# Stick-breaking attention: the running sums' products five units behind the softplus split instead of four, tiles five and six units apart

## The chip, the cores and the metric

The kernel runs on one core of one Trainium2 chip. The metric is the time of one execution in device microseconds; where a kernel is run several times, the median counts. A profiled execution stands beside these runs: its trace is what the sections below read.

## What is computed

One inference step of a one-layer hybrid decoder, for one prompt (16 meta tokens and 1024 tokens, together T = 1040) and for 8 sample sequences of 4 tokens with a paged cache. The input, normalised, goes through one shared input projection. Half of its columns feed a stick-breaking attention of 8 heads of size 128, the other half a gated linear attention; both go through gates and a shared output projection. The attention of the prompt is the part that the change touches. Its weights are not a softmax over keys but a product of "breaks", computed with running sums:

```python
def stick_break_weights(z, mask):
    sp = jnp.where(mask, jax.nn.softplus(z), 0.0)
    later = lax.cumsum(sp, axis=z.ndim - 1, reverse=True) - sp
    return jnp.where(mask, jnp.exp(jax.nn.log_sigmoid(z) - later), 0.0)

def sb_attend(qb, qpos, k, v, kpos, bias):
    a = stick_break_weights(sb_logits(qb, k, bias), kpos[None, :] < qpos[:, None])
    return jnp.einsum('bhqk,bkhd->bqhd', a.astype(v.dtype), v)
```

So key tile j of a block of queries needs the sum of the softplus values over all later key tiles: the tiles of one block form a chain, from the last key tile to the first.

All matrix products are made in fp32 accuracy out of three products of a number's two parts: the value rounded to the matmul's format (the "hi" part, a cast on ACT) and what is left of it (the "lo" part, a subtraction on DVE).

## The kernel before, in words

**Stages.** First the input is normalised and transposed; then come, head by head, the projections of the 8 attention heads with their attention woven in (from about 100 to 770 us); then the low-rank part of the gate and three groups of gate columns, with the last head's attention (to about 870 us); then the gated linear attention and the output projection. The attention of the sample sequences (its products and sums are the DVE instructions of L464, `jk`) is spread over DVE through all of it.

**Units.** A head's projection is `inproj` (L331), for v, then k, then q. Each has 8 loop steps over weights (a fresh weight chunk every second step: the hi cast on ACT at L182, the lo subtraction on DVE at L185), and each step has three column chunks of 384, 384 and 304 columns (for q 368, 384 and 304, without the 16 meta columns): six matmuls a chunk, L342 to L344 twice. After each chunk `W.beat()` runs. A chunk of six matmuls is one unit of the kernel's clock. A projection has 24 units and a head 72.

**Weaving.** `Weaver` (L53) holds generators with a due unit; at each beat it resumes those whose unit has come, and what they issue lands on the engines right behind the unit just made. The order on each engine follows that, but for steps marked `urgent` (weight casts, the projections' evacuations), which a scheduler may pull ahead as soon as their data are there.

**Attention.** Two units after head h's q projection, `attend` (L631) is started; it runs beside the projections of head h + 1. It starts 14 tiles, in the ORDER of L641: query block 1 (columns 528 to 1040, 512 queries) with key tiles 8 down to 0, then query block 0 with key tiles 4 down to 0. The tiles are numbered 0 to 13 in this order below. Their widths n are 32, 158, 284, 410 and five times 512 for block 1, then 24 to 512 (150, 276, 402, 512 among them) for block 0. The start of the next tile follows 2 to 5 units later, by n (L638).

A tile (`attend_tile`, L578) goes through these steps:

- z, three products (L589 to L591); DVE adds the bias and clips (L595); ACT exp and ln (L596, L597); DVE the maximum (L598): X is now the softplus. Where the diagonal passes through, POOL masks (L601). Then it waits 2 units.
- It waits until the previous tile of its block has set `carry`, units at a time. ACT copies the row of sums of the previous tile into row 0 of X (L607); `split_tmp` makes hi_s (ACT, L574) and lo_s (DVE, L575) out of X. Then it waits D1 units.
- The running sums' products: L610 (hi_s) and L611 (lo_s) add the triangular matrix's products to z. `carry` is set. ACT makes the weight Y (exp, L615); POOL masks (L617, diagonal tiles); hi_a and lo_a are split from Y. Then it waits D2 units.
- The three products with V into O (L623 to L625). The last tile of a block copies O to `ost` (ACT, L628) and stores it to DRAM (L629, `od`).

**Buffers.** X, Y and ost share three buffers (tag X), hi has three, lo has three, z has four. V, k and q of a head have one buffer each (a hi and a lo tile). So the reload of V for head h + 1 (`load_v`, L554: loads into staging tiles, three ACT copies L566 and three DVE subtractions L568) must wait for the last product with V of head h; the copies of head h + 1's k into its tile (`split_k`, ACT L693, DVE L694) must wait for the last z of head h; q is written by the evacuation of its projection (ACT L715, DVE L716, and L718 for the sample tokens). The projections' accumulators `acc` have three buffers: a chunk's next use waits for the evacuation of three chunks before.

**Queues.** Every engine works its instructions in the order in which they stand: ACT's and DVE's order around a tile is what the change moves. Weight loads, V's loads and the stores of od go through SP's queue.

Of the kernel before, what the change touches and what calls it, by code (L numbers as in the profile page):

```python
# [84 lines left out]
def hybrid_step(ctx: ExitStack, tc: tile.TileContext, x_prompt, x_sample, cache_k, cache_v, state_gla,  # L85
# [104 lines left out]
    with tc.tile_pool(name="xp", bufs=2) as xp, tc.tile_pool(name="xps", bufs=5, space=PSUM) as xps:  # L190
# [109 lines left out]
        for c, (lo, hi) in enumerate(XCHUNKS):  # L300
            n = hi - lo
# [225 lines left out]
    with tc.tile_pool(name="sp", bufs=1) as sp, tc.tile_pool(name="sps", bufs=1, space=PSUM) as sps:  # L527
# [103 lines left out]
        def attend(h, q, kt, V):  # L631

            carry, O = {}, {}
            for qi, j in ORDER:
                qlo, qhi = ((16, 528), (528, REAL))[qi]
                n = qhi - max(qlo, j * KT)
                W.spawn(attend_tile(h, qi, qlo, qhi, j, (qhi - 1) // KT, q, kt, V, carry, O))
                yield 2 if n < 100 else 3 if n < 200 else 4 if n < 450 else 5  # L638

        D1, D2 = 4, 6  # L640
        ORDER = [(1, j) for j in range(8, -1, -1)] + [(0, j) for j in range(4, -1, -1)]  # L641

        def values(h, behind):
# [19 lines left out]
        def head(h):  # L663
# [56 lines left out]
            inproj(C_SQ + h * P, ev_q, META, f"q{h}")  # L720
            V = values(h, copied[-1])
            W.spawn(attend(h, qt, kt, V), 2)

        W.spawn(z_feed(lambda n: 2), lasting=True)
# [946 lines left out]
def build(arrays_by_name):  # L1671
    import concourse.bacc as bacc
    nc = bacc.Bacc("TRN2", target_bir_lowering=False, num_devices=1, dynamic_dma_scratch_size=256)
    arrays, args = {}, []
    for name in _INS:
        a = arrays_by_name[name]
        arrays[f"in_{name}_dram"] = a
        args.append(nc.dram_tensor(f"in_{name}_dram", a.shape, mybir.dt.from_np(a.dtype), kind="ExternalInput").ap())
    for i, shape in enumerate(_OUTS):
        args.append(nc.dram_tensor(f"out_{i}_dram", shape, F32, kind="ExternalOutput").ap())  # L1680
    with tile.TileContext(nc) as tc:
        hybrid_step(tc, *args)
    return nc, arrays
# [8 lines left out]
```

## Time and profile before

| | |
|---|---|
| time, median of 3 runs | 2067.45 us (2066.13 to 2067.91) |
| the profiled execution's own time | 2066.38 us |
| its span, first to last instruction | 2064.6 us |
| mean granted TensorE clock | 0.999 |
| PE busy | 2024.8 us (98%) |
| PEld busy (weight loads) | 1863.6 us (90%) |
| DVE busy | 1552.7 us (75%) |
| ACT busy | 953.4 us (46%) |
| POOL busy | 84.6 us (4%) |

PE is TensorE's matmul part and PEld its weight load, which runs beside the matmul before it. Their shares say how full TensorE's queue is; a matmul's end is modelled, so that a stall shows as a longer distance from start to start, with only a part of it listed as idle time. The span leaves 2066.38 - 2064.6 = 1.78 us around it. The groups and rows of a view read `engine line operation output<-inputs shape`, with the time in us, and in square brackets the engine's idle time before it and what ended that.

### The profile page before, as it was taken

Reading aid. Unit: us, or ns where it says so; the run is one execution under the profiler, and the core shown is the slowest. Engines: PE = TensorE matmul, PEld = TensorE weight load, DVE = VectorE, ACT = ScalarE, POOL = GpSimd, SP = SyncE. Lnnn points to the kernel's source line nnn. Section 1 sums busy time; section 2 is a strip of 40 time slices with the busy share of each in tenths; the row PEclk is TensorE's granted clock in tenths of the full one; section 3 lists DMA queues with packets and bytes.
Section 4 is the critical chain, followed back from the end, with each engine's and each line's share of the span. In section 5 each row is a group of like instructions: output and inputs, shape, how many; then the busy total and the mean of one; then the engine's idle time right before and its main releaser. Section 6 shows DMA issues by size and latency. Waiting matters only on the chain.

```text
span 2064.6 us, 41985 instructions
## 1 busy us (share of the span) xinstructions
PE 2024.8 (98%) x12507; PEld 1863.6 (90%) x12507; DVE 1552.7 (75%) x6282; ACT 953.4 (46%) x2293; POOL 84.6 (4%) x304
## 2 busy tenths in 40 slices
PE   6999999999999999999999999999999999999998
PEld 5999999999999998999999999998888898788776
DVE  7368989888988989899798897978544347454576
ACT  7355555565655656433534335343433325332332
POOL 0012000101000000000000000000000000000000
PEclk9999999999999999999999999999999999999999
DMA  6354454544455442533433433335776666452485
GB/s 202 103 139 148 139 159 133 171 132 147 146 160 146 140 124 76 139 102 82 108 100 79 125 82 110 98 82 155 236 233 231 220 222 200 139 166 74 129 271 202
DMA packets 371821, 301.85 MB, mean 146 GB/s; under 512 B 42360, under 2 KB 312104, under 8 KB 371592
## 3 DMA queue, kind: packets, MB, share of 16 engines
q1 hardware_dynamic: 371288, 298.64, 48.6%
q8 instruction: 98, 1.61, 0.3%
q14 instruction: 131, 1.07, 0.2%
q10 hardware_dynamic: 304, 0.53, 0.1%
HBM read 241.75 MB, written 57.31 MB: 145 GB/s over the span
## 4 chain that ended last, share of the span: by engine, by line
PE 75%; DVE 12%; DMA 6%; ACT 3%; issue 3%; SPq 0%; POOL 0%; DVEq 0%; ACTq 0%; POOLq 0%
PE acc_g L342 5%; PE acc_g L343 5%; PE acc_g L344 5%; DVE jk L464 5%; PE b L1593 4%; PE b L1595 4%; PE b L1594 4%; PE acc_k L342 3%; PE acc_k L344 3%; PE acc_k L343 3%; PE acc_v L342 2%; PE acc_q L342 2%; PE acc_q L344 2%; PE acc_q L343 2%; PE acc_v L344 2%
## 5 line engine op out<-in xcount | busy, mean ns | idle before, releaser
L464 DVE SCALAR_TENSOR_TENSOR jk<-kp,qb 128x128 f32<-128x128 f32 x2048 | 593.8, 290 | 43.5 <-DMA qb<-qsd 1.7
L342 PE MATMUL acc_g<-hT,wh_g 128*128 128x368 f32 (+2 forms) x768 | 251.4, 327 | 0.5 <-DVE ga L389 0.5
L343 PE MATMUL acc_g<-hT,wh_g 128*128 128x368 f32 (+2 forms) x768 | 247.6, 322 | 0.0
L344 PE MATMUL acc_g<-hT,wl_g 128*128 128x368 f32 (+2 forms) x768 | 247.1, 322 | 0.0
L1593 PE MATMUL b<-ring,f 128*128 128x512 f32 x416 | 164.3, 395 | 3.5 <-ACT gx L521 1.4
L464 DVE DVE_READ_ACCUMULATOR jk<-kp,qb 128x1 f32 x2048 | 167.6, 82 | 0.0
L1594 PE MATMUL b<-ring,f 128*128 128x512 f32 x416 | 162.6, 391 | 0.0
L1595 PE MATMUL b<-ring,f 128*128 128x512 f32 x416 | 162.1, 390 | 0.0
L342 PEld LDWEIGHTS acc_g<-hT,wh_g 128*128 128x128 f32 x768 | 144.5, 188 | 13.3 <-issue 10.8
L343 PEld LDWEIGHTS acc_g<-hT,wh_g 128*128 128x128 f32 x768 | 144.6, 188 | 1.1 <-issue 0.4
L1395 DVE TENSOR_TENSOR ring<-wr,ring 128x512 fp32r<-128x512 f32 x104 | 71.3, 689 | 98.4 <-ACT ring L1394 97.7
L344 PEld LDWEIGHTS acc_g<-hT,wl_g 128*128 128x128 f32 x768 | 144.5, 188 | 0.0
L342 PE MATMUL acc_gv<-hT,wh_gv 128*128 128x400 f32 (+2 forms) x384 | 130.5, 340 | 0.0
L1394 ACT CAST ring<-wr 128x512 fp32r<-128x512 f32 x104 | 64.1, 620 | 139.3 <-PE b L1595 77.0
L342 PE MATMUL acc_k<-hT,wh_k 128*128 128x384 f32 (+1 forms) x384 | 126.4, 329 | 0.0
L343 PE MATMUL acc_gv<-hT,wh_gv 128*128 128x400 f32 (+2 forms) x384 | 125.3, 326 | 0.0
L342 PE MATMUL acc_q<-hT,wh_q 128*128 128x368 f32 (+2 forms) x384 | 125.1, 326 | 0.0
L344 PE MATMUL acc_gv<-hT,wl_gv 128*128 128x400 f32 (+2 forms) x384 | 124.8, 325 | 0.0
L344 PE MATMUL acc_k<-hT,wl_k 128*128 128x384 f32 (+1 forms) x384 | 124.7, 325 | 0.0
L343 PE MATMUL acc_k<-hT,wh_k 128*128 128x384 f32 (+1 forms) x384 | 124.5, 324 | 0.0
L344 PE MATMUL acc_q<-hT,wl_q 128*128 128x368 f32 (+2 forms) x384 | 123.4, 321 | 0.0
L343 PE MATMUL acc_q<-hT,wh_q 128*128 128x368 f32 (+2 forms) x384 | 123.4, 321 | 0.0
(454 smaller groups left out, 5294.3 us busy)
## 6 DMA issues: line engine op xcount, KB each, us to landing
kp<-in_cache_k_dram SPq DMA_DIRECT2D x512, 64.0 KB
vr<-in_cache_v_dram SPq DMA_DIRECT2D x64, 512.0 KB
tf<-in_w_out_dram SPq DMA_DIRECT2D x64, 256.0 KB
td<-tf SPq DMA_DIRECT2D x64, 256.0 KB
qb<-qsd SPq DMA_DIRECT2D x64, 256.0 KB
wr_g<-in_w_in_dram SPq DMA_DIRECT2D x64, 256.0 KB
wr<-td SPq DMA_DIRECT2D x56, 256.0 KB
wr<-in_w_out_dram SPq DMA_DIRECT2D x48, 256.0 KB
```

Source lines behind the costliest of these rows:

```text
L342: mm(acc[c][:, :n], wh, hh[k][:, lo:hi], start=(k == 0), stop=False)
L343: mm(acc[c][:, :n], wh, hl[k][:, lo:hi], start=False, stop=False)
L344: W.mark = mm(acc[c][:, :n], wl, hh[k][:, lo:hi], start=False, stop=(k == NK - 1)).ins
L464: ins = vec.scalar_tensor_tensor(jk[:], kp[:], 1.0, qbs[h, b][:, t, :], ALU.mult, ALU.mult, accum_out=zt[:, t, NPG - 1 - i:NPG - i])
L1394: act.copy(wh, r)
L1395: vec.tensor_tensor(wl, r, wh.bitcast(F32), ALU.subtract)
L1593: mm(bk[:], ah, wh, start=first and k == 0, stop=False, skip_group_check=True)
L1594: mm(bk[:], ah, wl, start=False, stop=False, skip_group_check=True)
L1595: mm(bk[:], al, wh, start=False, stop=last and k == 7, skip_group_check=True)
```

## The change

Two lines in `attend`: D1 is 5 instead of 4, and where the next tile started 4 or 5 units after a tile of at least 200 columns, it starts 5 or 6 units after it.

```diff
-                yield 2 if n < 100 else 3 if n < 200 else 4 if n < 450 else 5
+                yield 2 if n < 100 else 3 if n < 200 else 5 if n < 450 else 6
-        D1, D2 = 4, 6
+        D1, D2 = 5, 6
```

No instruction is added or removed on any engine; they stand in another order. With D1 = 5 the links of a block's chain are at least 5 units apart, and a head's last running sums and last products with V come at units 146 and 152, counted from the start of its v projection, where they came at 134 and 140. The next head's own first z is at unit 146 (two after its q projection) in both. So a head's last tiles now stand among the next head's first ones. Three places show what that does to ACT's and DVE's rows. Names carry head, query block and key tile: X2_1_8 is X of head 2, block 1, key tile 8 (tile 0); then comes a buffer number.

**First place: ACT, tiles 11 and 12 of head 1** (block 0, key tiles 2 and 1), with the copies of head 2's k (`k0_2`) and one weight cast between them. Before:

```order
L182 CAST wh_q2_2_4579<-wr_q2_2_4577 128x512
L693 CAST k0_2_3660<-kraw2_2_4259 128x114
L693 CAST k0_2_3660<-kraw2_2_4259 128x126
L693 CAST k0_2_3660<-kraw2_2_4259 128x32
L596 ACTIVATE X1_0_0_4418<-X1_0_0_4418 128x512
L545 COPY st_k2_2_4431<-tk_k2_2_4430 128x256
L597 ACTIVATE X1_0_0_4418<-X1_0_0_4418 128x512
L546 COPY st_k2_2_4431<-tk_k2_2_4430 48x128
L615 ACTIVATE Y1_0_2_4442<-z1_0_2_4176,bias0_827 128x276
L607 ACTIVATE X1_0_1_4311<-z1_0_2_4176 1x276
L574 CAST hi_a1_0_2_4445<-Y1_0_2_4442 128x276
L574 CAST hi_s1_0_1_4451<-X1_0_1_4311 128x402
```

After:

```order
L693 CAST k0_2_3643<-kraw2_1_4160 128x2x126
L693 CAST k0_2_3643<-kraw2_2_4204 128x114
L693 CAST k0_2_3643<-kraw2_2_4204 128x126
L693 CAST k0_2_3643<-kraw2_2_4204 128x32
L596 ACTIVATE X1_0_0_4574<-X1_0_0_4574 128x512
L597 ACTIVATE X1_0_0_4574<-X1_0_0_4574 128x512
L615 ACTIVATE Y1_0_2_4614<-z1_0_2_4324,bias0_827 128x276
L607 ACTIVATE X1_0_1_4472<-z1_0_2_4324 1x276
L574 CAST hi_a1_0_2_4617<-Y1_0_2_4614 128x276
L574 CAST hi_s1_0_1_4622<-X1_0_1_4472 128x402
L182 CAST wh_v3_0_4797<-wr_v3_0_4795 128x512
```

The copies of k stood ahead of tile 13's exp (L596 of X1_0_0); they still do. Y of tile 11 (L615 of Y1_0_2) and hi_s of tile 12 (hi_s1_0_1) follow in the same order; on PE, L610 and L611 of tile 12, which hi_s and lo_s feed, stand five units behind those of tile 11 instead of four. Tile 13's z was made at unit 125 and tile 11's L611 at 126; now they are made at 134 and 136.

**Second place: ACT, from head 1 to head 2**: the last ost of head 1, the evacuations of head 2's q, the copies of head 2's V (`V0_2`) and head 2's first tiles. Before:

```order
L628 COPY ost1_0_4731<-O1_0_4377 128x512
L715 ACTIVATE q0_2_4269<-acc_q2_0_4272 128x368
L715 ACTIVATE q0_2_4269<-acc_q2_1_4273 128x384
L182 CAST wh_v3_1_4967<-wr_v3_1_4965 128x512
L715 ACTIVATE q0_2_4269<-acc_q2_2_4274 128x272
L566 CAST V0_2_4808<-vr2_0_4825 128x384
L566 CAST V0_2_4808<-vr2_1_4856 128x384
L718 ACTIVATE qsm2_4271<-acc_q2_2_4274 128x32
L566 CAST V0_2_4808<-vr2_2_4896 128x384
L596 ACTIVATE X2_1_8_4865<-X2_1_8_4865 128x32
L597 ACTIVATE X2_1_8_4865<-X2_1_8_4865 128x32
```

After:

```order
L596 ACTIVATE X2_1_6_4995<-X2_1_6_4995 128x284
L597 ACTIVATE X2_1_6_4995<-X2_1_6_4995 128x284
L566 CAST V0_2_4790<-vr2_0_4807 128x384
L566 CAST V0_2_4790<-vr2_1_4847 128x384
L566 CAST V0_2_4790<-vr2_2_4890 128x384
L628 COPY ost1_0_5010<-O1_0_4529 128x512
L182 CAST wh_v3_3_5237<-wr_v3_3_5235 128x512
L615 ACTIVATE Y2_1_8_5022<-z2_1_8_4852,bias0_827 128x32
L607 ACTIVATE X2_1_7_4921<-z2_1_8_4852 1x32
L574 CAST hi_a2_1_8_5025<-Y2_1_8_5022 128x32
L574 CAST hi_s2_1_7_5050<-X2_1_7_4921 128x158
```

The copies of V and ost stood ahead of tile 0's exp; they now stand behind the ln of tile 2 (X2_1_6), with Y of tile 0 (Y2_1_8), the row of sums for tile 1 and hi_s of tile 1 behind them and behind a weight cast. Two of the three X buffers hold X2_1_7 and X2_1_6 at this place, whose splits are still to come, so that Y2_1_8 takes the third, which ost1_0 has until its store to DRAM has been read out. Before, Y2_1_8 stood 19 rows behind ost1_0; now it stands two behind it.

**Third place: DVE, the evacuations of head 2's q** (L716, `q1_2`), beside tiles 12 and 13 of head 1 and a weight's lo part (`wl_v3_1`). Before:

```order
L464 SCALAR_TENSOR_TENSOR jk0_1_2_3_4758,zt0_1_4675<-kp0_1_2_4549,qb0_1_4467 128x128
L489 TENSOR_TENSOR tf2_1_4332<-tf2_1_4332 128x512
L716 SCALAR_TENSOR_TENSOR q1_2_4270<-acc_q2_0_4272,q0_2_4269 128x368
L464 SCALAR_TENSOR_TENSOR jk0_1_3_0_4790,zt0_1_4675<-kp0_1_3_4589,qb0_1_4467 128x128
L464 SCALAR_TENSOR_TENSOR jk0_1_3_1_4792,zt0_1_4675<-kp0_1_3_4589,qb0_1_4467 128x128
L716 SCALAR_TENSOR_TENSOR q1_2_4270<-acc_q2_1_4273,q0_2_4269 128x384
L464 SCALAR_TENSOR_TENSOR jk0_1_3_2_4794,zt0_1_4675<-kp0_1_3_4589,qb0_1_4467 128x128
L489 TENSOR_TENSOR tf2_1_4332<-tf2_1_4332 128x512
L716 SCALAR_TENSOR_TENSOR q1_2_4270<-acc_q2_2_4274,q0_2_4269 128x272
```

After:

```order
L575 TENSOR_TENSOR lo_a1_0_1_4712<-Y1_0_1_4708,hi_a1_0_1_4711 128x402
L716 SCALAR_TENSOR_TENSOR q1_2_4215<-acc_q2_0_4217,q0_2_4214 128x368
L464 SCALAR_TENSOR_TENSOR jk0_1_2_1_4728,zt0_1_4646<-kp0_1_2_4499,qb0_1_4415 128x128
L575 TENSOR_TENSOR lo_s1_0_0_4736<-X1_0_0_4574,hi_s1_0_0_4735 128x512
L716 SCALAR_TENSOR_TENSOR q1_2_4215<-acc_q2_1_4218,q0_2_4214 128x384
L185 TENSOR_TENSOR wl_v3_1_4962<-wr_v3_1_4959,wh_v3_1_4961 128x512
L716 SCALAR_TENSOR_TENSOR q1_2_4215<-acc_q2_2_4219,q0_2_4214 128x272
L464 SCALAR_TENSOR_TENSOR jk0_1_2_2_4730,zt0_1_4646<-kp0_1_2_4499,qb0_1_4415 128x128
L489 TENSOR_TENSOR tf2_1_4283<-tf2_1_4283 128x512
L464 SCALAR_TENSOR_TENSOR jk0_1_2_3_4732,zt0_1_4646<-kp0_1_2_4499,qb0_1_4415 128x128
```

Before, only the sample attention's rows (L464, `jk`, and L489) stood between them, since the splits of tiles 12 and 13 were long done; now lo_a of tile 12 stands ahead of the first and lo_s of tile 13 ahead of the second.

## The prediction

> **What bounds the kernel now.** I read the page's busy shares first, then the waits of TensorE's two parts over the stretch that the change touches (100 to 870 us), then one of these waits in time, on every engine that takes part.
>
> ```profile
> PE 2024.8 (98%) x12507; PEld 1863.6 (90%) x12507; DVE 1552.7 (75%) x6282; ACT 953.4 (46%) x2293; POOL 84.6 (4%) x304
> PEclk9999999999999999999999999999999999999999
> ```
>
> TensorE is busy for 98% of the span at a full clock, and the change takes no matmul away. It can only win time in which TensorE stands. The two tables of waits say how much that is, first for the matmuls, then for the weight loads:
>
> ```profile
> PE z L611 <- DVE lo_s L575: 2.5, 9, 0.8
> PE z L610 <- ACT hi_s L574: 1.7, 4, 0.9
> PE acc_g L342 <- DVE ga L389: 0.5, 1, 0.5
> ```
>
> ```profile
> PEld z L611 <- DVE lo_s L575: 6.2, 13, 1.1
> PEld z L610 <- ACT hi_s L574: 3.3, 5, 1.2
> PEld acc_g L342 <- DVE ga L389: 0.7, 1, 0.7
> ```
>
> The columns are total us, number of waits, longest. All that TensorE waits for attention are the two splits of the softplus, the operands of L610 and L611: 4.2 us by the matmuls, 9.5 by the weight loads. Which of them the time pays shows in one event, in head 1 at tile 12 (matmuls, then weight loads):
>
> ```profile
> 284.25 0.33 PE L343 MATMUL acc_q<-hT,wh_q 128*128 128x368 f32 x1
> 284.42 0.32 PE L344 MATMUL acc_q<-hT,wl_q 128*128 128x368 f32 x1
> 284.83 0.45 PE L610 MATMUL z<-hi_s,ntri 128*128 128x402 f32 x1
> 285.45 0.45 PE L611 MATMUL z<-lo_s,ntri 128*128 128x402 f32 x1 [0.17 <-DVE lo_s L575]
> 285.74 0.34 PE L342 MATMUL acc_q<-hT,wh_q 128*128 128x384 f32 x1
> ```
>
> ```profile
> 284.83 0.19 PEld L610 LDWEIGHTS z<-hi_s,ntri 128*128 128x128 f32 x1 [0.39 <-ACT hi_s L574]
> 285.44 0.19 PEld L611 LDWEIGHTS z<-lo_s,ntri 128*128 128x128 f32 x1 [0.43 <-DVE lo_s L575]
> ```
>
> Undisturbed, the next 368-column matmul starts 0.17 us later; 402 columns are worth 0.17 x 402/368 = 0.19. Here the starts are 0.41 and 0.62 apart: 0.24 + 0.43 = 0.67 us lost, against 0.82 in the weight loads' rows and 0.17 in the matmuls'. So the price of all these waits is near 0.67/0.82 x 9.5 = 7.8 us; 4.2 and 9.5 are its bounds.
>
> Why the splits are late there, ACT's and DVE's rows show:
>
> ```profile
> 280.57 0.60 ACT L693 CAST k<-kraw 128x114 fp32r<-128x114 f32 x3
> 281.08 0.62 ACT L596 ACTIVATE X<-X 128x512 f32<-128x512 f32 x1
> 281.87 0.63 ACT L597 ACTIVATE X<-X 128x512 f32<-128x512 f32 x1
> 282.54 0.49 ACT L615 ACTIVATE Y<-z,bias 128x276 f32<-128x276 f32 x1
> 284.26 0.52 ACT L574 CAST hi_s<-X 128x402 fp32r<-128x402 f32 x1
> ```
>
> ```profile
> 284.81 0.58 DVE L575 TENSOR_TENSOR lo_s<-X,hi_s 128x402 fp32r<-128x402 f32 x1
> ```
>
> ACT works without a gap through the copies of the next head's k and tile 13's exp and ln before it comes to tile 11's Y at 282.54; the row of sums and hi_s follow, and lo_s ends at 285.39. This is a queue in front of a short chain, not a slow chain.
>
> **What the change does to it.** The distance between one L610 and the next grows from four units to five. A unit of six matmuls is 6 x 0.17 = 1.03 us, one of 304 columns 1.03 x 304/368 = 0.85. The longest wait in the tables is 1.2, so one unit takes away nearly all of each. At tile 12 there is more to it: tile 13's z comes one unit before tile 11's L611 in the old order and two units before it in the new one, so the work that held Y up has a further unit to drain. I take both rows at L610 and L611 as gone: -7.8 (bounds -4.2 and -9.5).
>
> What is added lies at the changes of head, seven of them. There tile 0's Y and tile 1's splits now follow the V copies and ost. These rows have the durations, and a tile 0 to tile 1 link from head 4 has the chain behind Y (ACT, then DVE):
>
> ```profile
> L566 ACT CAST V<-vr 128x384 fp32r<-128x384 f32 x24 | 11.1, 509 | 1.9 <-DMA vr<-out_dram 1.8
> L628 ACT COPY ost<-O 128x512 f32<-128x512 f32 x16 | 9.4, 586 | 16.0 <-PE O L625 15.8 <-DVE lo_a L575 0.2
> ```
>
> ```profile
> 498.00 0.27 ACT L615 ACTIVATE Y<-z,bias 128x32 f32<-128x32 f32 x1
> 498.77 0.32 ACT L574 CAST hi_s<-X 128x158 fp32r<-128x158 f32 x1
> ```
>
> ```profile
> 499.12 0.32 DVE L575 TENSOR_TENSOR lo_s<-X,hi_s 128x158 fp32r<-128x158 f32 x1
> ```
>
> From Y's start to lo_s's end it is 499.44 - 498.00 = 1.44 us. Let s be the start of the last product with V of a head. Tile 1's L611 stands six units behind it: four units of 1.03 and two of 0.85, that is 5.8 us, and with L625 itself (0.17 x 512/368 = 0.24), tile 3's three z products of 410 columns (3 x 0.19) and L610 it is due at about s + 6.7. On ACT the last product has ended by about s + 0.4; three V copies of 0.51 and ost of 0.59 take it to s + 2.5. Y must then wait until ost has been stored, since it gets ost's buffer. With a landing time L of that store, lo_s is ready at s + 2.5 + L + 1.44, and TensorE stands for L - 2.8 us where that is positive.
>
> L is what the trace does not have at this place. Three pairs of rows bound it (a store's issue on SP, and the instruction that waited for it or used its buffer):
>
> ```profile
> 852.62 0.32 SPq L629 DMA_DIRECT2D od<-ost  x1
> 856.52 0.30 ACT L800 CAST wal<-walr 96x128 fp32r<-96x128 f32 x1 [1.82 <-DMA od<-ost]
> ```
>
> ```profile
> 2056.47 0.33 SPq L1567 DMA_DIRECT2D out_dram<-og  x1
> 2058.74 1.67 POOL L1580 TENSOR_TENSOR y<-y,xr 128x512 f32<-128x512 f32 x1 [327.25 <-DMA out_dram<-og]
> ```
>
> ```profile
> 179.03 0.34 SPq L629 DMA_DIRECT2D od<-ost  x1
> 182.47 0.37 ACT L615 ACTIVATE Y<-z,bias 128x150 f32<-128x150 f32 x1
> ```
>
> The first store took 3.9 us to release its waiter, the second 2.3, and the third, in the middle of a head, at most 3.4, since Y shows no wait. So a head's change costs between 0 and 1.1 us. I take 2.8 for six of the seven, which is about the middle of 2.3 and 3.4 and costs nothing, and 3.9 for one: +1.1 in all (bounds 0 and 7 x 1.1 = 7.7).
>
> [...]
>
> Two smaller terms. The wait of L342 for `ga` (0.5 to 0.7 us in the rows above) lies at the end of the low-rank part, where tiles of head 7 now stand between what fills and what empties the accumulator: it about doubles, +0.5 (bounds 0 and 0.7). And in head 7 the last tiles of block 1 have their splits behind other work more closely than before; no row shows them waiting, and two waits of the size of the longest listed, 1.2, bound it: 0 to 2.4, taken as +1.0.
>
> The sum: -7.8 + 1.1 + 0.5 + 1.0 = -5.2. Against the profiled execution's 2066.38 that is 2061.2 us. The median of the runs lies 1.07 higher, at 2067.45: 2062.25 us for it. 0.2% of 2067.45 is 4.1 us, about what a measurement of this kernel can tell from no change.
>
> **The rivals.** *No change, because the stores give it back.* ACT works in order, and holds all behind an instruction that waits for a DMA; the trace has such a case, a V copy in head 4 with a short copy behind it that had nothing to do with it:
>
> ```profile
> 492.70 0.51 ACT L566 CAST V<-vr 128x384 fp32r<-128x384 f32 x1 [1.75 <-DMA vr<-out_dram]
> 493.12 0.17 ACT L658 COPY zns<-zn 32x32 f32<-32x32 f32 x1
> ```
>
> If each of the seven stores lands in 3.9 us, they cost 7.7 instead of 1.1: -7.8 + 7.7 + 1.5 = +1.4, so 2068.85 us. For it speaks that the landing of 3.9 is the only one of od which the trace shows to the end; against it the 3.4 in mid-head, where Y went into a stored ost's buffer without a wait. [...]
>
> *Slower, by the evacuation of q.* DVE's part of it (L716) now stands behind lo_a of tile 12 and lo_s of tile 13, and the accumulator that it frees is the next chunk's of the next head's v. The prices:
>
> ```profile
> L575 DVE TENSOR_TENSOR lo_s<-X,hi_s 128x512 fp32r<-128x512 f32 x48 | 32.9, 685 | 0.1
> L716 DVE SCALAR_TENSOR_TENSOR q<-acc_q,q 128x384 fp32r<-128x384 f32 x8 | 4.5, 558 | 0.5 <-ACT q L715 0.5
> L575 DVE TENSOR_TENSOR lo_a<-Y,hi_a 128x402 fp32r<-128x402 f32 x8 | 4.6, 574 | 0.0
> ```
>
> Where lo_a waits for its hi part, L716 waits with it. If both splits, 0.57 + 0.69 us, come on top of an evacuation that was just in time, a head loses 1.26 us, eight heads 10.1: -5.2 + 10.1 = +4.9, so 2072.35 us. It decides from about 0.9 us of lateness: two units lie between a chunk's last use for q and its accumulator's first for v, 1.03 + 0.85 = 1.88 us, and L716 with an ACT half of about its own length takes 1.0 of them. Against it: L342 of v shows no wait for L716 in the tables, and of the two splits ahead of L716 the second, lo_s of tile 13, needs nothing that is late.
>
> *The waits stay.* The k copies keep their place ahead of tile 13's exp in the new order, and move along with it. If Y of tile 11 is held up by a unit more as well, nothing at L610 and L611 is won, and the small terms remain: +1.1 + 1.5 = +2.6, so 2070.05 us. Against it stands that z of tile 13 comes two units ahead of L611 now.
>
> **How the numbers follow.** The forecast 0.50, 2062.25 us; its own range goes from -9.5 with no costs to -4.2 + 1.1 + 0.5 + 1.0 = -1.6, that is 2058 to 2066. No change by the stores 0.30, slower by q 0.15, the waits staying 0.05. Of the forecast's chance a tenth, 0.05, lies above 2063.3, where the gain is under 0.2%, and of the stores' case a tenth, 0.03, above 2071.6. Faster: 0.45. Within 0.2%: 0.05 + 0.27 + 0.05 = 0.37. Slower: 0.15 + 0.03 = 0.18. The range reaches from 2058.5 (-9.5 with 0.5 of the costs) to 2069.5 (the stores' case and half of the 1.4 by which it loses), and leaves out q's and, by a hair, the waits staying.
>
> **What would show it.** In the profile of the changed kernel, the rows of L610 and L611 among TensorE's waits should be under 1.5 us in the weight loads, with nothing left at tile 12. At the head changes, ACT's Y of tile 0 shows a wait for the od store or none, and L611 of tile 1 a wait of L - 2.8 us: that splits forecast and first rival. A row "L342 <- DVE q L716" would be q's. The prediction is wrong if PE's start-to-start distances lose time at a place that has none of these rows.

## The result, and the profile after

The changed kernel took 2094.11 us, the median of 4 runs (2090.34 to 2095.84), against 2066.79 us for the kernel before (2064.6 to 2067.91, 4 runs). The ratio is 1.0134, with a 95% interval of 1.0122 to 1.0146: slower by 27 us, where 5 us less were forecast and the range ended at 2069.5.

First the page of the changed kernel, in the rows that were shown of before:

```profile
PE 2034.4 (97%) x12507; PEld 1871.5 (89%) x12507; DVE 1553.1 (74%) x6282; ACT 957.4 (46%) x2293; POOL 86.5 (4%) x304
PEclk9999999999999999999999999999999999999999
```

The span went from 2064.6 to 2091.3 us. TensorE is busy 9.6 us longer with as many matmuls, so some of them took longer; the slices of the clock row are 52 us long and round this away. Next, what TensorE waits for from 100 to 900 us, by the matmuls (total us, number, longest):

```profile
PE z L610 <- ACT hi_s L574: 9.5, 5, 4.2
PE acc_v L342 <- DVE q L716: 4.6, 5, 2.4
PE z L611 <- DVE lo_s L575: 2.6, 5, 0.6
PE acc_gk L342 <- ACT gx L521: 2.1, 2, 1.1
PE acc_ga L374 <- DVE q L716: 1.3, 1, 1.3
PE acc_g L342 <- DVE ga L389: 0.4, 1, 0.4
```

Before, this list had three rows with 4.7 us. Now hi_s is waited for at other places, up to 4.2 us at once, and L716, the evacuation of q, is a row of its own. What hi_s waited for stands in ACT's list:

```profile
ACT Y L615 <- DMA od<-ost: 17.1, 6, 5.2
```

It is Y of tile 0 at the changes of head, and only that. The change from head 1 to head 2, on ACT, then on SP, then on TensorE:

```profile
314.35 0.58 ACT L628 COPY ost<-O 128x512 f32<-128x512 f32 x1
316.62 0.62 ACT L182 CAST wh_v<-wr_v 128x512 fp32r<-128x512 f32 x1 [1.69 <-PE acc_v L343]
321.82 0.29 ACT L615 ACTIVATE Y<-z,bias 128x32 f32<-128x32 f32 x1 [4.58 <-DMA od<-ost]
322.60 0.32 ACT L574 CAST hi_s<-X 128x158 fp32r<-128x158 f32 x1
```

```profile
314.46 0.37 SPq L441 DMA_DIRECT2D qb<-qsd  x1
314.95 0.42 SPq L629 DMA_DIRECT2D od<-ost  x1
315.61 0.34 SPq L485 DMA_DIRECT2D tf<-in_w_out_dram  x1
```

```profile
319.02 0.34 PE L344 MATMUL acc_v<-hT,wl_v 128*128 128x384 f32 x1
322.97 0.34 PE L610 MATMUL z<-hi_s,ntri 128*128 128x158 f32 x1 [3.61 <-ACT hi_s L574]
323.94 0.34 PE L611 MATMUL z<-lo_s,ntri 128*128 128x158 f32 x1 [0.63 <-DVE lo_s L575]
```

ACT stands 4.58 us for the store of ost, 6.9 us after SP issued it. Tile 1's hi_s, which has nothing to do with that store, stands behind it. TensorE starts L610 3.95 us after the matmul before it. And then it is not back at its pace: the granted clock in the four stretches behind such stops (start and end, length, busy us and instructions of PE, PEld, DVE, ACT, POOL, then the clock, DMA share and GB/s):

```profile
225.69:229.10 3.41, 3.41 (x12) 3.41 (x12) 3.03 (x17) 1.29 (x5) 0.58 (x2) 0.50 0.64 220
324.69:328.10 3.41, 3.41 (x14) 3.41 (x13) 3.14 (x19) 1.29 (x5) 0.58 (x2) 0.51 0.28 89
683.05:686.46 3.41, 3.41 (x12) 3.41 (x12) 3.21 (x11) 0.20 (x1) 0.00 (x0) 0.50 0.15 32
706.94:713.76 6.82, 6.23 (x22) 6.23 (x23) 5.02 (x29) 2.20 (x6) 0.59 (x2) 0.50 0.20 64
```

In 17.05 us the clock is at half, which costs 8.5. In the trace of before no half microsecond between 100 and 1000 us has less than the full clock.

A sum over the trace of what each distance between two matmul starts exceeds the median of its kind, from 100 to 910 us, puts this together. At L610 and L611 it was 7.5 us before and is 13.8 now. At L342 of the next head's v it was 0.5 and is 5.7. The halved stretches hold 8.9, the two waits for gx at 894 and 896 us 1.3. All in all the sum is 22.4 us larger. The first matmul of the gq projection, which follows the whole attention, starts at 919.67 us instead of 894.59, which is 25.1 later; 2.7 of them the sum leaves unassigned. About 2 of these are in TensorE's list above, the wait for q at L374 (1.3) and the rest of gx's 2.1: a distance that comes only a few times sets its own median, so the sum misses it.

### The profile page after: what moved, and what is told of

The parts are those of the page before. It is cut to its first block, busy times and chain, and to the rows that moved or that the text cites. A ratio compares the mean times of both kernels' runs of the same rounds, so it can differ in the third digit from the quotient of the medians.

```text
span 2091.3 us, 41960 instructions
## 1 busy us (share of the span) xinstructions
PE 2034.4 (97%) x12507; PEld 1871.5 (89%) x12507; DVE 1553.1 (74%) x6282; ACT 957.4 (46%) x2293; POOL 86.5 (4%) x304
## 4 chain that ended last, share of the span: by engine, by line
PE 63%; DVE 12%; DMA 8%; issue 3%; ACT 2%; SPq 1%; POOL 0%; DVEq 0%; ACTq 0%; POOLq 0%
DVE jk L464 5%; PE acc_g L342 5%; PE acc_g L343 5%; PE acc_g L344 5%; PE b L1593 4%; PE b L1595 4%; PE b L1594 4%; PE acc_k L342 2%; PE acc_k L343 2%; PE acc_k L344 2%; DMA qb<-qsd 2%; PE acc_v L342 2%; PE acc_gq L342 2%; PE acc_gq L343 2%; PE acc_gq L344 1%
## 5 line engine op out<-in xcount | busy, mean ns | idle before, releaser
L464 DVE SCALAR_TENSOR_TENSOR jk<-kp,qb 128x128 f32<-128x128 f32 x2048 | 591.9, 289 | 44.8 <-DMA qb<-qsd 1.7
L342 PE MATMUL acc_g<-hT,wh_g 128*128 128x368 f32 (+2 forms) x768 | 251.3, 327 | 0.4 <-DVE ga L389 0.4
L464 DVE DVE_READ_ACCUMULATOR jk<-kp,qb 128x1 f32 x2048 | 166.5, 81 | 0.0
L342 PEld LDWEIGHTS acc_g<-hT,wh_g 128*128 128x128 f32 x768 | 144.3, 188 | 13.3 <-issue 10.8
L342 PE MATMUL acc_gv<-hT,wh_gv 128*128 128x400 f32 (+2 forms) x384 | 130.4, 340 | 0.0
L342 PE MATMUL acc_q<-hT,wh_q 128*128 128x368 f32 (+2 forms) x384 | 126.6, 330 | 0.0
L342 PE MATMUL acc_k<-hT,wh_k 128*128 128x384 f32 (+1 forms) x384 | 125.4, 327 | 0.0
```

Source lines behind the costliest of these rows:

```text
L342: mm(acc[c][:, :n], wh, hh[k][:, lo:hi], start=(k == 0), stop=False)
L464: ins = vec.scalar_tensor_tensor(jk[:], kp[:], 1.0, qbs[h, b][:, t, :], ALU.mult, ALU.mult, accum_out=zt[:, t, NPG - 1 - i:NPG - i])
```

## The experiments

**A small buffer for narrow Y.** The theory after the result was that the store holds tile 0's Y, TensorE stands, and its clock halves behind that. One thing is taken away from the changed kernel: tiles of at most 32 columns get a Y of their own, 128 bytes a partition. TensorE's order in the trace is that of the changed kernel but for two matmuls.

```diff
-            yt = sp.tile([P, 512], F32, tag="X", bufs=3, name=f"Y{nm}")
+            yt = sp.tile([P, 512], F32, tag="X", bufs=3, name=f"Y{nm}") if n > 32 else sp.tile([P, 32], F32, tag="Yn", bufs=1, name=f"Y{nm}")
```

> The changed kernel with one thing else: the weight Y of the tiles of at most 32 columns (tile 0 and tile 9 of a head) has a small buffer of its own and no longer takes the one that the stored ost holds. Theory (the store of od holds tile 0's Y back, TensorE stands at tile 1, and its clock is halved behind it; q's evacuation adds a smaller part): ACT's wait of 17.1 us for od before L615 goes, the five stalls at tile 1 (13.5 us in the trace) and the three halved stretches behind them (3.4, 3.4 and 6.9 us, worth 6.9) go, so about 2094 - 20 = 2074 us, 2070 to 2078; q's stalls (4.6 us) and one halved stretch stay. Rival (tile 1 is late because V's copies and the weight casts stand in front of it, whatever the store does): 2085 to 2094, tile 1 still standing.

It took 2077.27 us (2073.53 to 2082.48), 1.0054 of the kernel before (1.0036 to 1.0073): 17 us of the 27 are gone. ACT's list has left of the store:

```profile
ACT Y L615 <- DMA od<-ost: 3.1, 2, 1.7
```

and TensorE's, of what it had:

```profile
PE acc_v L342 <- DVE q L716: 5.1, 5, 2.4
PE acc_gk L342 <- ACT gx L521: 2.4, 2, 1.3
PE acc_g L342 <- DVE ga L389: 1.6, 1, 1.6
PE acc_ga L374 <- DVE q L716: 1.2, 1, 1.2
PE z L611 <- DVE lo_s L575: 0.2, 1, 0.2
```

L610 is gone from the list, and of L611 0.2 us are left, at tile 12. The theory of the store holds, and the time lies in its range. One part of it missed: a halved stretch was to stay behind L716, and the clock is at 1.00 through the whole attention (the last section comes back to this). What is left in the list is L716 and the last head's end.

**The halves of the change alone.** D1 = 5 with the old starts, and D1 = 4 with the later starts.

```diff
-                yield 2 if n < 100 else 3 if n < 200 else 5 if n < 450 else 6
+                yield 2 if n < 100 else 3 if n < 200 else 4 if n < 450 else 5
```

> Only the first half of the change: D1 is 5, the tiles start four and five units apart as before. A head's last products with V then come one unit ahead of the next head's first z instead of six behind it. Theory (the loss is the overlap of a head's last tiles with the next head's first): no stall at tile 1, q's evacuation behind splits that are done, the waits at tile 12 mostly gone, 2060 to 2066 us. Rival (five units between split and products hold buffers longer and cost by themselves): slower than 2070.

```diff
-        D1, D2 = 5, 6
+        D1, D2 = 4, 6
```

> Only the second half of the change: D1 stays 4, tiles start five and six units apart. A head's last products with V come at the unit of the next head's first z. Theory (the loss is the overlap of heads): 2060 to 2067 us, tile 12's waits mostly gone because the wide tiles are five units apart. Rival (the later starts cost by themselves, since V's copies move to the next head's first tiles here too): 2075 or more with stalls at tile 1.

D1 alone took 2076.92 us, a ratio of 1.0043 (1.0029 to 1.0057); the starts alone 2076.18 us, 1.0034 (1.0021 to 1.0048). Both theories failed: neither half has a stall at tile 1, but each is slower than before, with a time in its rival's range. ACT's Y waits for the same buffer at another place. Its groups of L615 that waited for the store, in D1 alone, then in the starts alone:

```profile
L615 ACT ACTIVATE Y<-z,bias 128x276 f32<-128x276 f32 x8 | 3.9, 492 | 21.7 <-DMA od<-ost 18.1 <-PE acc_q L344 3.6
```

```profile
L615 ACT ACTIVATE Y<-z,bias 128x24 f32<-128x24 f32 x8 | 2.3, 281 | 17.4 <-DMA od<-ost 17.4
```

In mid-head ost of block 1 is stored too. Before the change, no Y waited for it. With D1 = 5 it meets the Y of 276 columns (tile 11), with the later starts the Y of 24 (tile 9). With both it is the store of block 0 and the Y of 32 (tile 0). Each of the three orders puts another Y behind a store. For the later starts a run below takes this wait away, and the loss goes with it. For D1 = 5 alone no run does: its waits at L610 and L611 come to 5.0 us in TensorE's list against 4.2 before, the rest is spread over waits for other rows of ACT (3.6) and one halved stretch. That the 18.1 us behind the store are the cause is not shown.

**A longer wait at one tile, for the clock.** In the kernel before, ACT copies X of one tile per head onto itself, several times, ahead of hi_s.

```diff
+            for _ in range((0, 3, 4, 5, 6, 7, 8, 10)[h] if (qi, j) == (1, 3) else 0):
+                act.copy(X, X)
             sh, sl = split_tmp(X, nk, n, "s" + nm)
```

> The kernel before with TensorE made to stand once a head: at tile 5, ACT copies X onto itself 0, 3, 4, 5, 6, 7, 8 and 10 times (heads 0 to 7) ahead of hi_s, which changes no value. Theory (a standing TensorE has its clock halved for a stretch of 3.4 us afterwards): waits from none to about 5 us, the clock at 1.00 behind the short ones and at 0.50 for 3.4 us or a multiple behind those of 2.5 us and more. Rival (the halved stretches of the changed kernel came from something else): the granted clock stays at 1.00 behind all of them, and each costs only its own length.

One run took 2073.27 us. The longest wait that this made was far from the 5 us meant; TensorE's list:

```profile
PE z L612 <- ACT hi_s L574: 4.4, 9, 0.9
PE z L613 <- DVE lo_s L575: 3.0, 9, 0.8
```

(L612 and L613 are L610 and L611, two lines down.) The order on TensorE had moved along with the slower tile, so that the copies were mostly covered. The clock stayed at 1.00 behind all of these. For waits of up to 0.9 us that fits the theory, and it decides nothing for longer ones.

**The store on another queue.** Why did the store take 7 us, twice as long as the rows of before allowed?

```diff
-                nc.sync.dma_start(od[h][:, qlo - META:qhi - META], st[:])
+                nc.scalar.dma_start(od[h][:, qlo - META:qhi - META], st[:])
```

> The changed kernel with the stores of od issued on ACT's queue instead of SP's; nothing else differs in the source. The store took 2.1 to 7.0 us from its issue to tile 0's Y. Theory (the long ones stood behind the transfers issued just ahead of them on SP's ring, a 256 KB load of qb above all): on a ring of its own the store lands in 2 to 3.5 us at every change of head, and the stalls of 3.8 and 4.4 us at tile 1 shrink to under 1.5; about 2080 us. Rival (all 16 DMA engines are busy with those loads, whatever ring a store comes from): landings up to 5 us and more stay, and the time stays at 2088 or more.

2085.3 us (2 runs, 1.0092, 1.0073 to 1.011). The change from head 1 to head 2, on ACT:

```profile
316.01 0.33 ACTq L629 DMA_DIRECT2D od<-ost  x1
317.75 0.62 ACT L182 CAST wh_v<-wr_v 128x512 fp32r<-128x512 f32 x1 [1.77 <-PE acc_v L343]
322.80 0.29 ACT L615 ACTIVATE Y<-z,bias 128x32 f32<-128x32 f32 x1 [4.43 <-DMA od<-ost]
```

6.8 us from issue to Y, as before on SP's queue (6.9). Over the seven changes of head it was 2.1, 6.8, 3.9, 4.7, 2.1, 5.1 and 2.2 us, against 2.1, 6.9, 2.9, 4.7, 2.1, 7.0 and 2.4. SP's ring is not what holds it. The rival's landings held; the time lay between the two forecasts. The rival's reason, that the 16 DMA engines are busy, is not what the trace shows. Their share (the number before the last) in half a microsecond behind the slow store at 314.95, then behind the one at 600.84, which landed in 2.1 us:

```profile
317.00:317.50 0.50, 0.50 (x5) 0.50 (x4) 0.44 (x4) 0.24 (x1) 0.00 (x0) 1.00 0.25 78
602.00:602.50 0.50, 0.50 (x6) 0.50 (x5) 0.43 (x5) 0.05 (x1) 0.00 (x0) 1.00 1.01 381
```

What the slow ones have in common is a load of qb (L441) on SP's queue. In the changed kernel and in this run, it was issued 0.1 to 1.2 us ahead of each of the three slowest stores of the seven, and not within 3 us ahead of the other four. No run moved that load, so it is not shown to be the cause; in D1 alone ACT's longest wait for a store, in mid-head, was 4.8 us. Of the 9 us that the kernel gained (6.6 between the two profiled executions), TensorE's stalls at tile 1 are 4.0 (9.5 us in its trace against 13.5, 3.2 of it in the one change whose landing went from 7.0 to 5.1) and the halved stretches 1.7 (four of 3.4 us).

**The later starts with the small buffer.** The starts' half, without its wait: the changed kernel with the buffer shown above and

```diff
-        D1, D2 = 5, 6
+        D1, D2 = 4, 6
```

> D1 4 and the later starts, with the small buffer for the Y of narrow tiles: the waits for od in the run with the later starts alone were all at tile 9's Y (24 columns, 17.4 us), and this buffer takes it out of their way. Theory (the store of ost holds the buffer of whichever Y comes next, here in mid-head): the 6.9 us at L610 and the two halved stretches (3.4) go, 2076.2 - 10 = 2066 us, level with the kernel before or a little faster. Rival (the later starts cost by the splits' place): 2072 or more.

2063.14 us (11 runs, 2060.89 to 2065.07) against 2067.0 (15 runs), 0.9982 (0.9973 to 0.9991): faster than the kernel before. TensorE's list:

```profile
PE z L611 <- DVE lo_s L575: 2.0, 5, 0.5
PE acc_g L342 <- DVE ga L389: 0.7, 1, 0.7
PE z L610 <- ACT hi_s L574: 0.4, 1, 0.4
```

ACT's list has no Y waiting for the store, and L716 is not in TensorE's. The gain is small because L611 still waits, now at tile 13.

**Later heads.** The changed kernel with the small buffer, each head's attention two units later, so that L716 stands ahead of lo_a of tile 12:

```diff
-            W.spawn(attend(h, qt, kt, V), 2)
+            W.spawn(attend(h, qt, kt, V), 4)
```

> The changed kernel with the small buffer for narrow Y, and a head's attention started four units after its predecessor's projection instead of two, so that DVE has L716, the evacuation of q, ahead of lo_a of tile 12 and lo_s of tile 13 in its order. Theory (q's stall comes from standing behind those splits): TensorE's wait of 5.1 us for L716 goes, and the run is about 5 us below the one with the small buffer alone, 2072. Rival (DVE is behind by a few us there whatever the order): the wait for L716 stays or moves to the splits, 2076 or more.

2081.45 us, 1.0071 (1.0052 to 1.009), no better than with the small buffer alone (1.0054, 1.0036 to 1.0073). The wait for L716 at v did go, but another evacuation, one of ACT's, took its place:

```profile
PE acc_k L342 <- ACT vraw L666: 6.9, 6, 2.1
PE acc_gk L342 <- ACT gx L521: 3.4, 1, 3.4
```

Moving L716 forward moved the wait to another place and did not remove it. Why ACT is late there, this run does not show.

**DVE with less to do.** The sample attention's rows (L464) fed every third unit instead of every second, in the changed kernel with the small buffer; they come later then, in stages that have no room for them.

```diff
-        W.spawn(z_feed(lambda n: 2), lasting=True)
+        W.spawn(z_feed(lambda n: 3), lasting=True)
```

> The changed kernel with the small buffer for narrow Y, and the sample attention's products on DVE (L464) fed every third unit instead of every second; they are all still made, later ones in later stages. Theory (L716 is late because DVE is some 2 us behind with L464 rows that stand ahead of lo_a of tile 12): TensorE's wait of 5.1 us for L716 shrinks to under 1.5 in the attention stretch, whatever the later stages then lose. Rival (the place behind lo_a and lo_s alone does it): it stays at 4 or more.

2201.6 us in all, 1.065 (1.0631 to 1.0668), from the stages behind. The attention is what this run was for. TensorE's list from 100 to 900 us:

```profile
PE acc_v L342 <- DVE q L716: 0.4, 2, 0.2
PE acc_g L342 <- DVE ga L389: 0.3, 1, 0.3
PE z L611 <- DVE lo_s L575: 0.2, 1, 0.2
```

The first matmul of the gq projection, in the kernel before, then in this one:

```profile
894.59 0.34 PE L342 MATMUL acc_gq<-hT,wh_gq 128*128 128x384 f32 x1
```

```profile
886.86 0.34 PE L342 MATMUL acc_gq<-hT,wh_gq 128*128 128x384 f32 x1
```

With the order of the change, but DVE less loaded, the attention ends 7.7 us earlier than before, and 12.7 earlier than with the small buffer alone (899.61), with the same order on TensorE but for two matmuls. DVE's load from 200 to 600 us, in the kernel with the small buffer, then in this one (the third pair is DVE):

```profile
200.00:600.00 400.00, 397.29 (x2439) 384.03 (x2438) 360.47 (x1649) 228.10 (x549) 38.68 (x121) 1.00 0.52 148
```

```profile
200.00:600.00 400.00, 399.82 (x2464) 388.19 (x2464) 308.10 (x1242) 231.77 (x556) 38.52 (x123) 1.00 0.48 137
```

90% against 77%. The old order was not run with this feed, so the 7.7 us need not all be the order's.

**Last products a unit earlier.** The later starts with the small buffer, and

```diff
-        D1, D2 = 4, 6
+        D1, D2 = 4, 5
```

> The version with D1 4, the later starts and the small buffer for narrow Y, and D2 5 instead of 6, so that the products with V and the end of a head come one unit earlier. Theory (a later end of the head is what collides with the next one): level with that version or up to 3 us faster, 2060 to 2063 us. Rival (the products with V then wait for lo_a): TensorE waits at L623 or L624, 2066 or more.

2064.31 us, 0.9992 (0.9983 to 1.0): no better, and the rival's wait at L623 did not come either. (One of its 12 executions took 11404 us; the median does not feel it.)

**A slower feed for the attention stretch alone**, one step in four, first in the changed kernel with the small buffer, then with D1 = 4:

```diff
-        W.spawn(z_feed(lambda n: 2), lasting=True)
+        W.spawn(z_feed(lambda n: 3 if n < 288 and n % 4 == 0 else 2), lasting=True)
```

> The changed kernel with the small buffer for narrow Y, and one in four of the first 288 steps of the sample attention fed a unit later (2.25 units a step instead of 2, for the attention stretch alone). Theory (DVE at 90% is what makes q's evacuation and the splits late at a change of head): DVE a tenth less loaded, TensorE's waits for L716 down to 1 to 3 us from 5.1, the attention stretch at most level with the kernel before; in all 2062 to 2070 us if the later stages take the rest of the sample work without waiting. Rival (the later stages have no room): slower than 2080.

> The same feed with the version of D1 4, later starts and the small buffer. Theory: its remaining waits at tile 13 and in the last head (5 us in the weight loads) shrink, 2058 to 2063 us. Rival (the later stages have no room): slower than 2070.

2118.7 us (1.0259, 1.0242 to 1.0276) and 2103.22 us (1.0182, 1.0165 to 1.0199). The rival held in both: the later stages have no room, one wait there alone is this long (first kernel, from 900 us on):

```profile
PE acc_g L342 <- ACT gx L521: 20.3, 1, 20.3
```

In the attention DVE went to 86% from 200 to 600 us, and the wait for L716 to 4.3 us from 5.1, more than the forecast 1 to 3. With this order, the point where it goes lies between 86 and 77%.

## Why the prediction was wrong

**What bounds the kernel, and the price of the old waits: right.** The waits at L610 and L611 were priced at 7.8 us from one event; the sum of start-to-start distances in the trace gives 7.5. With the new order and the small buffer, 0.2 us of them are left by the matmuls and 1.1 of 9.5 by the weight loads. So the first term, -7.8, was earned, or nearly. It was given back.

**The step that failed is the landing time L of the store.** The working had the right chain, up to "TensorE stands for L - 2.8 us". Of seven landings it took six at 2.8 us and one at 3.9, and 3.9 as the most. Measured they were 2.1 to 7.0. The stalls at tile 1 by TensorE's starts are 1.6, 4.6, 0.7, 1.4, 0, 5.2 and 0 us, 13.5 together, where +1.1 was taken and 7.7 was the upper end. With the measured landings the prediction's own formula gives 10.3 of the 13.5, so it is in the main the size of L that was wrong, and not the chain. The three rows were no sample of the place: none of them had a load of qb issued within 3 us ahead, as the store at 314.95 has at 314.46. Why L is 7 us there stays open. Four of the seven landings, 2.1 to 2.9 us, are near the 2.3 of the second of these rows; 6.9 and 7.0 are near none.

A smaller error in the same step makes half of the rest: the chain from Y to lo_s was taken as 1.44 us from one row in head 4. At 222.07 us Y starts and the stall comes to 1.6 us, though this store landed in 2.1: a weight's lo part and rows of L464 stood ahead of lo_s on DVE.

**What the prediction did not have: the clock.** It read the granted clock as full and priced each stop by its own length. The halved stretches add 8.5 us: 6.8 behind the stalls at tile 1, half as much again as the stalls themselves, and 1.7 behind a wait for L716. No row of before has a halved stretch in the attention: the longest distance there was 1.1 us over the normal (before L610 at 192.19 us), and the clock is at 1.00 behind it. In the changed kernel a pair of stops of 0.7 and 0.9 us over the normal distance, at 223 us, already has 3.41 us at 0.50 behind it. That the stop is what halves the clock is read from the order of events in these traces; the run that was to test it made no wait of over 0.9 us.

**The rivals were priced one at a time.** The store, q's evacuation and the last head's end all happened in one run. q's was put at 10.1 us for being late in all heads, with "needs nothing that is late" against it; it came to 5.7 us, in seven places. Its deciding point (0.9 us) was passed because DVE works through L464 rows that stand ahead of lo_a. Tile 12 of head 5 and the q of head 6 in the changed kernel show it, ACT first, then DVE (the first row is the last of six of L464):

```profile
678.23 0.53 ACT L574 CAST hi_a<-Y 128x402 fp32r<-128x402 f32 x1
678.67 0.47 ACT L715 ACTIVATE q<-acc_q 128x368 fp32r<-128x368 f32 x1
```

```profile
680.87 0.29 DVE L464 SCALAR_TENSOR_TENSOR jk<-kp,qb 128x128 f32<-128x128 f32 x1
681.09 0.68 DVE L489 TENSOR_TENSOR tf<-tf 128x512 f32<-128x512 f32 x1
681.69 0.57 DVE L575 TENSOR_TENSOR lo_a<-Y,hi_a 128x402 fp32r<-128x402 f32 x1
682.18 0.53 DVE L716 SCALAR_TENSOR_TENSOR q<-acc_q,q 128x368 fp32r<-128x368 f32 x1
```

hi_a is done at 678.76 and q's first half at 679.14; DVE comes to them at 681.69 and 682.18. TensorE waits 2.4 us for it. Before the change, too, DVE was 89% busy from 200 to 600 us, and the price of q's evacuation has no term for what stands ahead of it on such an engine. The run with 77% shows that this matters (0.4 us of waits instead of 5.1). But the load alone does not decide it: with D1 = 4 and the small buffer DVE is busy for 91% of the same stretch, and TensorE's list has no row for L716:

```profile
200.00:600.00 400.00, 398.75 (x2446) 385.45 (x2445) 363.71 (x1653) 231.58 (x552) 37.37 (x121) 1.00 0.53 149
```

It took the order of the change and a full DVE together.

**The last head.** +1.5 was taken for `ga` and for head 7's splits. The splits show no stop of over 0.5 us there. The rows for gx, ga and q at the low-rank part come to 3.8 us (2.1, 0.4 and 1.3); gx was not among the terms.

**The signs.** Faster, same and slower had 0.45, 0.37 and 0.18. The mechanism with the second highest chance, 0.30, was the one that decided, with a price that stopped at "no change".

## What to carry to other kernels

Before an order is shifted, ask of each buffer ring which instruction gets the buffer that a store is still reading: here each of the three new orders put another Y behind it, and 128 bytes of its own for a 32-column tile were worth 17 us. A DMA's landing is bounded by rows from the same place, not by others: here the rows gave 2.3 to 3.9 us, and the place had 2.1 to 7.0. On an engine as busy as DVE is here (88 to 91% from 200 to 600 us), ask what a new order puts ahead of a step that others wait for. And in the sum, a stop of TensorE can cost more than its length: here 1.6 us in two stops already had 3.41 us at half the clock behind them, another 1.7 us.

## What the runs showed of the hardware

The halved stretches of the changed kernel begin at 225.69, 324.69, 683.05 and 706.94 us; three are 3.41 us long and one 6.82. Counted from the first, the starts are 29, 134 and 141 times 3.413 us (481.25 us / 141): in this trace the clock went to half on a fixed grid. The run with the store on ACT's queue has four stretches of 3.41 us, which by its half microseconds begin at 301.71, 325.60, 684.00 and 704.48 us: 7, 112 and 118 times 3.413 us from the first. Not every stop had such a stretch behind it. The same wait for L716 in head 6 was 2.39 us in the changed kernel and was followed by a halved stretch; with the small buffer it was 2.37 us, and the clock behind it stayed full:

```profile
670.64 0.45 PE L342 MATMUL acc_v<-hT,wh_v 128*128 128x384 f32 x1 [2.37 <-DVE q L716]
```

```profile
670.60:674.00 3.40, 3.36 (x18) 2.99 (x19) 3.37 (x12) 0.46 (x2) 0.00 (x0) 1.00 0.17 37
```

Steps of 3.413 us laid over the changed kernel's trace from its halved stretches, with what the distances of matmul starts exceed the normal one added up in each step, show where these stops fall. Of the steps at full clock between 100 and 900 us, those from 321.23, 679.63 and 703.52 us hold 2.7, 2.7 and 3.3 us and were followed by a halved one. The one from 222.24, with the pair of stops, holds 1.7 us and was too; the one from 317.82 holds 2.0 us and was not, nor was any other, of which none holds more than 1.4. The wait at tile 1 that ends at 322.97 us is cut at 321.23: the step with its first part was followed by a full one, that with its rest by a halved one. Before the change no 3.413 us, wherever laid, hold more than 1.6 us, and the clock stays full. How the wait of 2.37 us with the small buffer falls into such steps is not shown: from 100 to 997 us no stretch of that trace is halved. What else decides whether a step is halved, these runs don't settle. Halved stretches are probably why the changed kernel with the small buffer spreads from 2073.5 to 2082.5 us over four runs: the two near 2073.7 have a mean granted clock of 0.998, that of 2080.61 has 0.994 and that of 2082.48 has 0.996, and a thousandth is some 2 us. There is a trace of one of the faster two alone (2073.93), without a halved stretch in the attention.
